# Hybrid delta-net and window-attention block on one Trainium2 core: x's loads behind the branches, decays moved, last norm in two passes, and two projections that pass once over their weights

## The chip, the cores and the metric

The kernel runs on 1 core of one Trainium2 chip. The metric is device time in microseconds (us) of one execution. The profiled execution is one run of the program with the hardware profiler; its rows give, for each instruction, the engine, the start and the duration. Engines: PE is TensorE (matmuls; PEld is its weight load), DVE is VectorE, ACT is ScalarE, POOL is GpSimd, SP is SyncE, whose queue issues nearly all transfers.

## The reference

One layer over 2048 tokens of width 1024, in float32, with two causal mixers side by side:

```
h = x @ w_in                                   # q, k, v, z, beta, decay | q, k, v, z | 2 gates
a: q,k,v = silu(short_conv(h)); gated delta rule in chunks (4 heads of 128)
   u, w come from the inverse of a unit lower triangular matrix per chunk
   o_a = rmsnorm(o_a) * silu(z)
b: 8 query heads of 64, 2 key heads, rope on a quarter, window of 128, a sink per head
   o_b = softmax(band) @ v * silu(z)
merged = sigmoid(gate_a) * (o_a @ w_branch[0]) + sigmoid(gate_b) * (o_b @ w_branch[1])
y = layernorm(alpha * x + merged @ w_out) * ln_g + ln_b
```

## The kernel before

The sequence goes in four chunks of 512 tokens. In the code `T` is 512 and `NB` is 4, the blocks of 128 tokens in a chunk; `KT` is 8, the blocks of 128 along the width. Every large product is made of three fp32r matmuls (L179, L180, L181 in `prods`): each operand is split into a high part and a low part, and high by high, high by low and low by high are summed in PSUM. I call such a group of three a triple.

**Weights and x.** In chunk 0 a weight quarter comes raw from HBM (L159), ACT rounds it to its high part (L160), DVE subtracts (L161), and the split form is stored to a scratch tensor `kw_...` (L145); the later chunks load that form (L156). There are three raw buffers (`W_RAW`) and four split buffers `wb` (`W_SPLIT`). x of the next chunk takes the same raw buffers (`load_x`, L217 to L219).

**Order.** PE's order is written by hand. The strings `ORDER_FIRST` and `ORDER` list the dense pieces of a chunk (`kv`, `w0`, `w1` the query projections, `g` gates, `p` the output projection of the chunk before, and so on). Between them stand background tasks, spawned with a latency (`LAT_...`) on a model clock: `front`, `levels`, `back` of a delta-rule head, `attend` of the window attention, `decays`. The class `Order` puts a step of such a task into PE's stream when the model clock has passed its due time. `st.finish(name)` moves the model clock on until the named task is done, so that its steps then stand back to back. The other engines' orders are made by a list scheduler.

**What the change touches.**
- `decays` makes the decay tables from `ba`: cumulative sums with two matmuls (L293, L294), four small transposes (L308) and a row form `GT` of 8 rows. `front` spreads a row of `GT` over 128 partitions with one matmul (L382) whose stationary operand is `sel`.
- `back` is a serial chain over the four blocks of a head: L504, DVE L506, L509, DVE L511, L512 and L515, DVE L516, L517, and the next block's L504 needs the state that L516 wrote. Dense triples between them cover the trips to DVE.
- `attend` makes for each block the scores (L598, L599), a softmax on DVE and ACT (L606 to L618), transposes of it (L625) and the product with v (L633).
- `window_q` projects queries, block pair by block pair: the four weight quarters are kept in `wb` for the second pair. Rope (L889 on ACT, L893 to L895 on DVE) follows, then `query_rows` transposes (L572). `project` does the same for the output projection with weights `kw_o`.
- `inverse` is a chain on DVE (L943, L944) between transfers: L404 to L406 out and in, L432 to `scrp`, L445 back as `p_` for L457.
- `last_project` ends the program with the last chunk's output projection and its norm: L757, statistics, POOL's power (L878), L764 on DVE beside L762 on ACT, L765, and L766 on POOL for one half and DVE for the other.
- `start` splits the first x and the first three weights as they arrive.

Of the kernel before, what the change touches and what calls it, by code (L numbers as in the profile page):

```python
# [39 lines left out]
LAT_INV, LAT_B, LAT_S, LAT_N, LAT_SM, LAT_D, LAT_M, LAT_K, LAT_Q, LAT_Y, LAT_F, LAT_W = 29600, 2700, 2300, 7700, 9200, 11000, 9000, 1400, 7900, 8300, 4100, 2300  # L40
# [23 lines left out]
def build(tc, xt, xn, wk, wg, par, lnp, cst, out, seq=2048):  # L64
    nc = tc.nc
    NCH = seq // T
    with ExitStack() as ctx:
# [67 lines left out]
        sel = const.tile([8, NH], F32R, name="sel")  # L135
        nc.vector.tensor_copy(sel, selt)
# [37 lines left out]
        def prods(ps, terms, first=True, last=True):  # L174

            n = len(terms) - 1
            cost = PE_R * ps.free_size() / 512
            for i, (sh, sl, mh, ml) in enumerate(terms):
                nc.tensor.matmul(ps, sh, mh, start=(first and i == 0), stop=False)  # L179
                nc.tensor.matmul(ps, sh, ml, start=False, stop=False)  # L180
                nc.tensor.matmul(ps, sl, mh, start=False, stop=(last and i == n))  # L181
                if cost * 3 * (i % 2 + 1) > 1000 or i == n:
                    yield cost * 3 * (i % 2 + 1)
# [12 lines left out]
        def prod_tc(pss, blocks, ah, al, ww, load=None):  # L196

            for g, (wh, wl) in enumerate(ww):
                if load:
                    load(2 * g + 1)  # L200
                for ps, b in zip(pss, blocks):
                    yield from prods(ps, [(tok(ah[2 * g + k], b), tok(al[2 * g + k], b), wh[:, k], wl[:, k])
                                          for k in range(2)], g == 0, g == 3)

        def kept(ww, into):
            for w in ww:
                into.append(w)
                yield w
# [14 lines left out]
        def start(c):  # L223
# [6 lines left out]
            for k in range(KT):  # L230
# [6 lines left out]
                if not k % 4:  # L237
                    wb = [pw.tile([P, 2, 528], F32R, name="wb", bufs=W_SPLIT)[:, :, :512] for _ in FIRST]
                    wh, wl = ([b[:, n] for b in wb] for n in range(2))
                    for i in range(3):  # L240
                        nc.vector.tensor_copy(wh[i], first[i + 3 * (k // 4)])
                        nc.vector.tensor_tensor(wl[i], first[i + 3 * (k // 4)], wh[i].bitcast(F32), ALU.subtract)
                        keep((FIRST[i], k // 4), wb[i])
# [41 lines left out]
        def decays(c, ba):  # L285
# [23 lines left out]
            c.GT = sm.tile([8, T], F32R, name="GT", bufs=1)  # L309
            nc.scalar.activation(c.GT, psr[:8], AF.Copy)  # L310
# [45 lines left out]
        def front(c, h):  # L356
# [25 lines left out]
            nc.tensor.matmul(psR, sel[:, h:h + 1].to_broadcast([8, P]), c.GT, start=True, stop=True)  # L382
# [165 lines left out]
        def window_q(c, gp):  # L548
# [4 lines left out]
            ww, more = [], quarters([f"q{gp}{i}" for i in range(2)])  # L553
            for b0 in (0, 2):
                pss = [mm.tile([P, T], F32, name="mm")[:, :256] for _ in range(2)]
                yield from prod_tc(pss, (b0, b0 + 1), c.xh, c.xl, ww if b0 else kept(more, ww), lambda k: load_x(c, k))
                if b0:
                    st.finish("qT0")
                qr = [pa.tile([P, 256], F32, name="kr") for _ in range(2)]
                for b, ps in enumerate(pss):  # L560
                    rope(nc, sm, qr[b], ps, 4, cos[:, c.i * NB + b0 + b], sin[:, c.i * NB + b0 + b])
                st.spawn(f"qT{b0}", query_rows(c, b0, qr), LAT_Q)
# [114 lines left out]
        def project(c, eg):  # L677
# [3 lines left out]
            ww, more = [], quarters([f"o{eg}{i}" for i in range(2)])  # L681
# [6 lines left out]
            for b2 in range(2):  # L688
                yield from prod_tc([ps[:, b2] for ps in pss], (b2, 2 + b2), c.mh, c.ml, ww if b2 else kept(more, ww))
# [3 lines left out]
        def norm_factors(c, bst, bufs=None):  # L693
# [6 lines left out]
            if bufs:  # L700
                return rs, mv[:, 0:1]
            nm = sm.tile([P, 1], F32, name="lnm")
            nc.vector.scalar_tensor_tensor(nm, mv[:, 0:1], -1.0, rs, ALU.mult, ALU.mult)
            return rs, nm

        def layer_norm(c):
            fs = []
            for b in range(NB):
# [4 lines left out]
                rs, mu = norm_factors(c, bst, NB)  # L713
# [20 lines left out]
        def last_project(c):  # L734
# [9 lines left out]
            for b in range(NB):  # L744
# [51 lines left out]
        for i in range(NCH):  # L796
# [223 lines left out]
```

## Time and profile before

| what | us |
|---|---|
| median of 3 runs | 1695.29 (1693.77 to 1695.6) |
| profiled execution, its own time | 1688.99 |
| its span in the profile | 1687.2 |
| PE busy | 1619.6 (96% of the span) |
| DVE busy | 976.0 (58%) |
| ACT busy | 600.8 (36%) |
| POOL busy | 88.9 (5%) |

The profile page counts an engine as busy while one of its instructions runs. PE's matmuls are pipelined and their ends are modelled, so the distance from one start to the next tells more than a duration. The column PEclk is the share of TensorE's full clock that was granted; 0.5 is the lower of its two levels.

### The profile page before, as it was taken

What the parts mean: (1) busy time and instruction counts of PE and PEld (TensorE: products, weight loads), DVE (VectorE), ACT (ScalarE), POOL (GpSimd) and SP (SyncE); (2) the same over time, 40 slices, a digit from 0 to 9 for tenths busy, and PEclk for the clock granted to TensorE, in tenths of its full rate; (3) what the DMA queues carried; (4) which work ended last, traced back from release to release, by engine and by line L of the source; (5) the groups of instructions that cost most, each with busy time, mean ns of one, the idle gap of its engine ahead of it and who ended that gap; (6) DMA issues with size and microseconds to landing.
All of it is one profiled execution on the core that took longest, in us unless ns stands there. A gap on an engine that the chain in (4) does not pass through costs nothing.

```text
span 1687.2 us, 26971 instructions
## 1 busy us (share of the span) xinstructions
PE 1619.6 (96%) x9846; PEld 1366.6 (81%) x9846; DVE 976.0 (58%) x3015; ACT 600.8 (36%) x1692; POOL 88.9 (5%) x138
## 2 busy tenths in 40 slices
PE   9999999899899999999999999999999999999997
PEld 6878877787788778788888778878888878888787
DVE  6676686548748665433746774623482867462255
ACT  4464456424313633432311453333230244233110
POOL 0100000000001001000000000000000100000001
PEclk9999999999989999999999999999999999999999
DMA  8866584676857446556655835645656664464862
GB/s 307 265 223 198 180 272 154 207 237 218 280 199 221 133 145 176 157 146 224 197 178 182 245 120 150 178 144 176 207 176 193 221 185 122 149 197 138 285 207 76
DMA packets 189157, 323.37 MB, mean 192 GB/s; under 512 B 31072, under 2 KB 45408, under 8 KB 188896
## 3 DMA queue, kind: packets, MB, share of 16 engines
q1 hardware_dynamic: 185184, 316.40, 59.3%
q0 software_dynamic: 3840, 5.25, 1.5%
q8 instruction: 78, 1.28, 0.3%
q14 instruction: 55, 0.45, 0.1%
HBM read 244.97 MB, written 71.37 MB: 187 GB/s over the span
## 4 chain that ended last, share of the span: by engine, by line
PE 79%; DMA 8%; DVE 8%; ACT 2%; issue 1%; SPq 1%; POOL 0%; DVEq 0%; ACTq 0%
PE mm L179 22%; PE mm L181 21%; PE mm L180 21%; PE pp L633 2%; DMA s<-in_lnp 2%; PE pp L625 1%; DMA wb<-kw_o 1%; DMA w<-in_wg 1%; DMA wb<-kw_zb 1%; PE pp L598 1%; PE pd L509 1%; PE pd L504 1%; PE pd L393 1%; PE pp L599 1%; DMA wb<-kw_b 1%
## 5 line engine op out<-in xcount | busy, mean ns | idle before, releaser
L179 PE MATMUL mm<-xh,wb 128*128 128x512 f32 x1128 | 467.1, 414 | 2.0 <-DMA wb<-kw_zb 1.6
L181 PE MATMUL mm<-xh,wb 128*128 128x512 f32 x1128 | 445.4, 395 | 0.0
L180 PE MATMUL mm<-xl,wb 128*128 128x512 f32 x1128 | 444.2, 394 | 0.0
L179 PEld LDWEIGHTS mm<-xh,wb 128*128 128x128 f32 x1128 | 213.1, 189 | 50.3 <-issue 8.9
L181 PEld LDWEIGHTS mm<-xh,wb 128*128 128x128 f32 x1128 | 212.3, 188 | 49.9
L180 PEld LDWEIGHTS mm<-xl,wb 128*128 128x128 f32 x1128 | 213.8, 190 | 38.0
L179 PE MATMUL mm<-wb,xh 128*128 128x256 f32 (+1 forms) x384 | 115.1, 300 | 3.2 <-DVE rope L893 2.9
L179 PE MATMUL mm<-wb,s 128*128 128x256 f32 x384 | 112.1, 292 | 5.5 <-DMA wb<-kw_o 5.3
L180 PE MATMUL mm<-wb,xh 128*128 128x256 f32 (+1 forms) x384 | 109.1, 284 | 0.0
L181 PE MATMUL mm<-wb,s 128*128 128x256 f32 x384 | 109.0, 284 | 0.0
L180 PE MATMUL mm<-wb,s 128*128 128x256 f32 x384 | 108.9, 284 | 0.0
L181 PE MATMUL mm<-wb,xl 128*128 128x256 f32 (+1 forms) x384 | 108.6, 283 | 0.0
L161 DVE TENSOR_TENSOR wb<-w,wb 128x512 fp32r<-128x512 f32 (+1 forms) x110 | 75.7, 690 | 56.2 <-ACT wb L160 53.9
L160 ACT ACTIVATE wb<-w 128x512 fp32r<-128x512 f32 (+1 forms) x110 | 68.9, 628 | 84.8 <-PE mm L181 47.2
L179 PEld LDWEIGHTS mm<-wb,s 128*128 128x128 f32 x384 | 73.6, 192 | 8.3 <-DMA wb<-kw_o 5.2
L943 DVE TENSOR_TENSOR xt<-su,xi 128x16 f32<-128x16 f32 (+15 forms) x256 | 76.4, 298 | 5.4
L179 PEld LDWEIGHTS mm<-wb,xh 128*128 128x128 f32 x384 | 73.2, 191 | 5.8 <-issue 5.4
L944 DVE TENSOR_REDUCE xi<-xt 128x8 f32<-128x16 f32 (+15 forms) x256 | 74.8, 292 | 5.1
L611 ACT ACTIVATE s<-s,nm 128x256 f32<-128x256 f32 (+1 forms) x128 | 62.6, 491 | 39.8 <-DVE nm L608 39.8
L180 PEld LDWEIGHTS mm<-wb,s 128*128 128x128 f32 x384 | 73.6, 192 | 0.1
L181 PEld LDWEIGHTS mm<-wb,s 128*128 128x128 f32 x384 | 73.5, 192 | 0.0
L317 ACT ACTIVATE xs<-mm 128x512 f32<-128x512 f32 x45 | 26.8, 596 | 131.0 <-PE mm L181 129.7
(665 smaller groups left out, 3045.6 us busy)
## 6 DMA issues: line engine op xcount, KB each, us to landing
wb<-kw_h SPq DMA_DIRECT2D x96, 512.0 KB, 4.1
wb<-kw_g SPq DMA_DIRECT2D x96, 512.0 KB, 3.9
w<-in_wg SPq DMA_DIRECT2D x106, 256.0 KB, 4.1
wb<-kw_b SPq DMA_DIRECT2D x48, 512.0 KB, 4.1
wb<-kw_o SPq DMA_DIRECT2D x36, 512.0 KB, 4.5
kw_h<-wb SPq DMA_DIRECT2D x32, 512.0 KB, 3.9
kw_g<-wb SPq DMA_DIRECT2D x32, 512.0 KB, 3.4
wb<-kw_q SPq DMA_DIRECT2D x24, 512.0 KB, 3.9
```

The lines of the kernel that those rows point to most:

```text
L160: nc.scalar.activation(hi, raw, AF.Copy)
L161: nc.vector.tensor_tensor(lo, raw, hi.bitcast(F32), ALU.subtract)
L179: nc.tensor.matmul(ps, sh, mh, start=(first and i == 0), stop=False)
L180: nc.tensor.matmul(ps, sh, ml, start=False, stop=False)
L181: nc.tensor.matmul(ps, sl, mh, start=False, stop=(last and i == n))
L317: nc.scalar.activation(xs[:, 3:], ps, AF.Copy)
L393: nc.tensor.matmul(psKK[:, b], k4[:, b], k4[:, b], start=True, stop=True)
L504: nc.tensor.matmul(ps, k4[:, b], S[:, h], start=True, stop=True)
L611: nc.scalar.activation(ss[v][:, g, k0:], ss[v][:, g, k0:], AF.Exp, bias=nm[:, v, g:g + 1], scale=0.125, accum_out=su[:, v, g:g + 1])
L633: nc.tensor.matmul(psY[64 * v:64 * v + 64], c.vs[b + kb][:, 64 * v:64 * v + 64], pTs[v][:, kb], start=(kb == kbs[0]), stop=(kb == 1))
L943: nc.vector.tensor_tensor(tx[:, :, :, :n], u, x, ALU.mult)
L944: nc.vector.tensor_reduce(xi[:, :, i:i + 2], tx[:, :, :, :n], AX.X, ALU.add)
```

## The change

Five things change. The query projection `window_q` and the output projection `project` go once over their four weight quarters (`prod_all`): each quarter is multiplied with all four token blocks, two blocks to a PSUM bank, with all four sums open. The next chunk's x is loaded one piece behind each `branch_b` product, and no longer all in front of them. `decays` becomes due later (`LAT_Y` 11500 for 8300), and `sel` and `GT` have 128 rows, of which 120 are zero. The last norm takes two fused DVE passes per half, without ACT and POOL. In `start` POOL makes the low parts of the first weights in place of DVE.

```
-LAT_INV, LAT_B, LAT_S, LAT_N, LAT_SM, LAT_D, LAT_M, LAT_K, LAT_Q, LAT_Y, LAT_F, LAT_W = 29600, 2700, 2300, 7700, 9200, 11000, 9000, 1400, 7900, 8300, 4100, 2300
+LAT_INV, LAT_B, LAT_S, LAT_N, LAT_SM, LAT_D, LAT_M, LAT_K, LAT_Q, LAT_Y, LAT_F, LAT_W = 29600, 2700, 2300, 7700, 9200, 11000, 9000, 1400, 7900, 11500, 4100, 2300
...
-        sel = const.tile([8, NH], F32R, name="sel")
-        nc.vector.tensor_copy(sel, selt)
+        sel = const.tile([P, NH], F32R, name="sel")
+        GT = const.tile([P, T], F32R, name="GT")
+        for t in (sel, GT):
+            nc.gpsimd.memset(t.bitcast(F32), 0.0)
+        nc.vector.tensor_copy(sel[:8], selt)
...
+        def prod_all(pss, ah, al, ww, load=None):
+            for g, (wh, wl) in enumerate(ww):
+                if load:
+                    load(2 * g + 1)
+                for b in (0, 2, 1, 3):
+                    yield from prods(pss[b // 2][:, b % 2], [(tok(ah[2 * g + k], b), tok(al[2 * g + k], b), wh[:, k], wl[:, k])
+                                                             for k in range(2)], g == 0 and not b % 2, g == 3, True)
...
-                        nc.vector.tensor_tensor(wl[i], first[i + 3 * (k // 4)], wh[i].bitcast(F32), ALU.subtract)
+                        nc.gpsimd.tensor_tensor(wl[i], first[i + 3 * (k // 4)], wh[i].bitcast(F32), ALU.subtract)
...
-            c.GT = sm.tile([8, T], F32R, name="GT", bufs=1)
-            nc.scalar.activation(c.GT, psr[:8], AF.Copy)
+            nc.scalar.activation(GT[:8], psr[:8], AF.Copy)
...
-            nc.tensor.matmul(psR, sel[:, h:h + 1].to_broadcast([8, P]), c.GT, start=True, stop=True)
+            nc.tensor.matmul(psR, sel[:, h:h + 1].to_broadcast([P, P]), GT, start=True, stop=True)
...
-            ww, more = [], quarters([f"q{gp}{i}" for i in range(2)])
+            pss = [mm.tile([P, 2, 256], F32, name="mm") for _ in range(2)]
+            yield from prod_all(pss, c.xh, c.xl, quarters([f"q{gp}{i}" for i in range(2)]), lambda k: load_x(c, k))
             for b0 in (0, 2):
-                pss = [mm.tile([P, T], F32, name="mm")[:, :256] for _ in range(2)]
-                yield from prod_tc(pss, (b0, b0 + 1), c.xh, c.xl, ww if b0 else kept(more, ww), lambda k: load_x(c, k))
                 if b0:
                     st.finish("qT0")
...
-            for b2 in range(2):
-                yield from prod_tc([ps[:, b2] for ps in pss], (b2, 2 + b2), c.mh, c.ml, ww if b2 else kept(more, ww))
+            yield from prod_all(pss, c.mh, c.ml, quarters([f"o{eg}{i}" for i in range(2)]))
...
-                rs, nm = norm_factors(c, bst)
-                for hs in (slice(0, 512), slice(512, D)):
-                    if hs.start:
-                        nc.scalar.activation(r[:, hs], r[:, hs], AF.Identity, scale=rs, bias=nm)
-                    else:
-                        nc.vector.tensor_scalar(r[:, hs], r[:, hs], rs, nm, ALU.mult, ALU.add)
-                    nc.vector.tensor_tensor(r[:, hs], r[:, hs], lg[:, 0, hs], ALU.mult)
-                    (nc.vector if hs.start else nc.gpsimd).tensor_tensor(r[:, hs], r[:, hs], lg[:, 1, hs], ALU.add)
+                rs, mu = norm_factors(c, bst)
+                halves = slice(0, 512), slice(512, D)
+                for hs in halves:
+                    nc.vector.scalar_tensor_tensor(r[:, hs], r[:, hs], mu, lg[:, 0, hs], ALU.subtract, ALU.mult)
+                for hs in halves:
+                    nc.vector.scalar_tensor_tensor(r[:, hs], r[:, hs], rs, lg[:, 1, hs], ALU.mult, ALU.add)
                     nc.sync.dma_start(out=out[t0:t0 + P, hs], in_=r[:, hs])
...
-            if i < NCH - 1:
-                load_x(nxt, KT - 1)
             for d in range(KT):
                 st.dense([branch_b(c, d)])
+                if i < NCH - 1:
+                    load_x(nxt, d)
```

In the changed kernel the line numbers are higher by 5 to 13: the triple is L184 to L186, the chain of `back` is L517, L522, L525, L528, L530, the scores are L610 and L611, the softmax's transposes L637, the query transposes L584.

SP's queue at the branches of chunk 0 stands so before (in_xt is x, in_wg a raw weight, kw_b the store of a split one):

```order
L145 DMA kw_g14_1_3674<-wb_3669 256x1x512
L217 DMA w_3752<-in_xt 128x512
L145 DMA kw_g15_0_3696<-wb_3691 256x1x512
L217 DMA w_3756<-in_xt 128x512
L145 DMA kw_g15_1_3729<-wb_3724 256x1x512
L217 DMA w_3762<-in_xt 128x512
L217 DMA w_3766<-in_xt 128x512
L217 DMA w_3772<-in_xt 128x512
L217 DMA w_3776<-in_xt 128x512
L217 DMA w_3782<-in_xt 128x512
L217 DMA w_3786<-in_xt 128x512
L159 DMA w_3791<-in_wg 128x512
```

With the change the same place reads:

```order
L163 DMA w_3730<-in_wg 128x512
L149 DMA kw_g15_0_3682<-wb_3677 256x1x512
L231 DMA w_3752<-in_xt 128x512
L149 DMA kw_g15_1_3707<-wb_3702 256x1x512
L163 DMA w_3757<-in_wg 128x512
L149 DMA kw_b0_1_3734<-wb_3729 256x1x512
L231 DMA w_3791<-in_xt 128x512
L149 DMA kw_b1_1_3761<-wb_3756 256x1x512
L163 DMA w_3796<-in_wg 128x512
L231 DMA w_3823<-in_xt 128x512
L163 DMA w_3828<-in_wg 128x512
```

The first weight of the branches stood behind eight loads of x; now it stands ahead of them, and x and weights take turns.

PE at the second query projection of chunk 1 stands so before, at the end of the projection (128x256 triples) and the start of the next product (128x512):

```order
L504 MATMUL pd<-S,k 128x128
...
L181 MATMUL mm<-wb,xl 128x256
L572 MATMUL pp<-ct,kr 128x128 x4
L509 MATMUL pd<-bt,q__6404 128x128
L512 MATMUL pd<-S,qd 128x128
L179 MATMUL mm<-xh,wb 128x512
...
L181 MATMUL mm<-xh,wb 128x512
L515 MATMUL pd<-wc,ktl 128x128
```

With the change it reads:

```order
L186 MATMUL mm<-wb,xl 128x256
L522 MATMUL pd<-bt,q__6439 128x128
L525 MATMUL pd<-S,qd 128x128
L528 MATMUL pd<-wc,ktl 128x128
L530 MATMUL pd<-wc,dt 128x128
L517 MATMUL pd<-S,k 128x128
L584 MATMUL pp<-ct,kr 128x128 x4
L522 MATMUL pd<-bt,q__6439 128x128
L525 MATMUL pd<-S,qd 128x128
L184 MATMUL mm<-xh,wb 128x512
```

Four triples stood between L504 and L509 and four more between L512 and L515; now five steps of the chain follow one another with only the transposes L584 between.

PE in chunk 1 ahead of `k3`, where the head's chain is finished, stands so before, from the last product ahead of the softmax's transposes (between the scores and this piece stand ten triples and two links of the chain):

```order
L181 MATMUL mm<-xh,wb 128x512
L504 MATMUL pd<-S,k 128x128
L625 MATMUL pp<-ct,s 128x128 x8
L509 MATMUL pd<-bt,q__5700 128x128
L512 MATMUL pd<-S,qd 128x128
L633 MATMUL pp<-pT,vb 64x256 x4
L515 MATMUL pd<-wc,ktl 128x128
L517 MATMUL pd<-wc,dt 128x128
```

With the change, from the last score on:

```order
L611 MATMUL pp<-kTl_145,qT_5520 128x256
L184 MATMUL mm<-xh,wb 128x512
...
L186 MATMUL mm<-xh,wb 128x512
L517 MATMUL pd<-S,k 128x128
L522 MATMUL pd<-bt,q__5694 128x128
L525 MATMUL pd<-S,qd 128x128
L528 MATMUL pd<-wc,ktl 128x128
L530 MATMUL pd<-wc,dt 128x128
L637 MATMUL pp<-ct,s 128x128 x4
```

Two triples are now between the last score and the head's last block, and that block's chain and the first transposes follow without a dense product between. Chunks 2 and 3 have the same piece.

## Rows read from the trace of the kernel before

**Rows 1.** The page, part 1: busy us (share of span) xinstructions.

```profile
PE 1619.6 (96%) x9846; PEld 1366.6 (81%) x9846; DVE 976.0 (58%) x3015; ACT 600.8 (36%) x1692; POOL 88.9 (5%) x138
```

**Rows 2.** PE's waits: us in total, times, longest us.

```profile
PE pd L457 <- DMA p__4900<-scrp: 8.4, 1, 8.4
PE mm L179 <- ACT wb L160: 7.2, 1, 7.2
PE mm L179 <- DMA wb<-kw_o: 5.3, 7, 1.9
PE pd L509 <- DVE bt L506: 5.3, 6, 1.5
PE pd L464 <- DVE q__968 L450: 3.6, 1, 3.6
PE mm L179 <- DVE rope L893: 2.9, 1, 2.9
PE pd L382 <- DVE ktl L372: 2.6, 4, 1.1
PE pd L293 <- DVE gg L922: 2.6, 1, 2.6
PE pd L457 <- DMA p__2747<-scrp: 2.4, 1, 2.4
...
PE mm L179 <- DMA wb<-kw_zb: 1.6, 2, 0.9
...
PE pp L598 <- DVE x__2861 L459: 1.2, 1, 1.2
...
PE pd L478 <- ACT x__2861 L451: 0.9, 1, 0.9
```

**Rows 3.** Stretches: us, then busy of PE, PEld, DVE, ACT, POOL, PEclk, DMA share.

```profile
44.00:54.00 10.00, 7.10 (x47) 6.93 (x47) 7.45 (x38) 3.58 (x13) 1.54 (x3) 0.83 0.91 314
119.00:132.00 13.00, 9.03 (x66) 7.34 (x65) 6.86 (x30) 7.63 (x25) 1.54 (x2) 0.87 0.29 88
245.00:262.00 17.00, 12.01 (x93) 9.04 (x92) 10.41 (x32) 10.13 (x35) 0.20 (x1) 0.87 0.45 144
332.00:345.00 13.00, 5.85 (x23) 4.64 (x22) 5.71 (x9) 5.30 (x9) 0.00 (x0) 0.74 0.67 215
```

**Rows 4.** SP's timeline at chunk 0's branches: start, us, line, transfer, times.

```profile
323.13 12.63 SPq L217 DMA_DIRECT2D w<-in_xt  x6
336.03 4.46 SPq L159 DMA_DIRECT2D w<-in_wg  x3
```

**Rows 5.** PE's timeline around the first L382: start, us, line, shape.

```profile
64.67 0.39 PE L180 MATMUL mm<-xl,wb 128*128 128x512 f32 x1
64.90 0.39 PE L181 MATMUL mm<-xh,wb 128*128 128x512 f32 x1
65.22 0.49 PE L382 MATMUL pd<-GT,sel 8*128 8x512 f32 x1
65.64 0.50 PE L179 MATMUL mm<-xh,wb 128*128 128x512 f32 x1
```

**Rows 6.** PE and DVE timelines, a link of `back` in chunk 2.

```profile
985.39 0.49 PE L504 MATMUL pd<-S,k 128*128 128x128 f32 x2
986.12 0.34 DVE L506 SCALAR_TENSOR_TENSOR bt<-pd,neG,vt 128x128 f32<-128x128 f32 x1
```

**Rows 7.** The timeline from the last score of a block to its softmax, chunk 1.

```profile
577.39 0.28 PE L599 MATMUL pp<-kTl,qT 128*128 128x256 f32 x1
584.13 1.70 ACT L618 ACTIVATE s<-s,sum 128x256 f32<-128x256 f32 x4
```

**Rows 8.** The chain that ended last, its end: start us, us, what.

```profile
1679.25 0.17 DVE lnm L703
...
1680.03 1.30 DVE yBl L765 x2
1681.33 0.02 issue
1681.35 1.63 DVE yBl L766
```

**Rows 9.** POOL's addition in the last norm: duration ns min/median/max, first and last start.

```profile
L766 POOL TENSOR_TENSOR yBl<-yBl,yAh x2: 1641/1660/1680, 1670.5 to 1680.8; 128x512 f32<-128x512 f32 x2
```

More of the change, by code (lines that the diff above doesn't have):

```diff
@@ L172, in quarters, with prods @@
                     yield half_w(name, i, 2)
-        def prods(ps, terms, first=True, last=True):
+        def prods(ps, terms, first=True, last=True, shared=False):
             n = len(terms) - 1
@@ L178, in prods @@
             for i, (sh, sl, mh, ml) in enumerate(terms):
-                nc.tensor.matmul(ps, sh, mh, start=(first and i == 0), stop=False)
-                nc.tensor.matmul(ps, sh, ml, start=False, stop=False)
-                nc.tensor.matmul(ps, sl, mh, start=False, stop=(last and i == n))
+                nc.tensor.matmul(ps, sh, mh, start=(first and i == 0), stop=False, skip_group_check=shared)
+                nc.tensor.matmul(ps, sh, ml, start=False, stop=False, skip_group_check=shared)
+                nc.tensor.matmul(ps, sl, mh, start=False, stop=(last and i == n), skip_group_check=shared)
                 if cost * 3 * (i % 2 + 1) > 1000 or i == n:
@@ L559, in window_q @@
                 qr = [pa.tile([P, 256], F32, name="kr") for _ in range(2)]
-                for b, ps in enumerate(pss):
-                    rope(nc, sm, qr[b], ps, 4, cos[:, c.i * NB + b0 + b], sin[:, c.i * NB + b0 + b])
+                for b in range(2):
+                    rope(nc, sm, qr[b], pss[b0 // 2][:, b], 4, cos[:, c.i * NB + b0 + b], sin[:, c.i * NB + b0 + b])
                 st.spawn(f"qT{b0}", query_rows(c, b0, qr), LAT_Q)
@@ L680, in project @@
                 c.ra = [py.tile([P, 2, D], F32, name=n) for n in ("yBh", "yBl")]
-            ww, more = [], quarters([f"o{eg}{i}" for i in range(2)])
             es = slice(256 * eg, 256 * eg + 256)
@@ L687, in project, with norm_factors @@
                 nc.sync.dma_start(out=xr[bp], in_=xn[t0:t0 + 256, es].rearrange("(b p) e -> p b e", p=P))
-            for b2 in range(2):
-                yield from prod_tc([ps[:, b2] for ps in pss], (b2, 2 + b2), c.mh, c.ml, ww if b2 else kept(more, ww))
+            yield from prod_all(pss, c.mh, c.ml, quarters([f"o{eg}{i}" for i in range(2)]))
             for bp in range(2):
                 nc.vector.scalar_tensor_tensor(c.ra[bp][:, :, es], xr[bp], 2.0 * ALPHA, pss[bp], ALU.mult, ALU.add)
-        def norm_factors(c, bst, bufs=None):
+        def norm_factors(c, bst):
             mv = sm.tile([P, 2], F32, name="mv", bufs=NB)
@@ L699, in norm_factors @@
             rsqrt(nc, sm, rs, va, mhalf)
[L700 to L704, printed above, removed]
+            return rs, mv[:, 0:1]
         def layer_norm(c):
@@ L712, in layer_norm @@
                     nc.vector.bn_stats(bst[:, i], r[:, 512 * i:512 * i + 512])
-                rs, mu = norm_factors(c, bst, NB)
+                rs, mu = norm_factors(c, bst)
                 fs.append((r, rs, mu))
@@ L758, in last_project @@
                         nc.vector.bn_stats(bst[:, e0 + e], r[:, es])
-                rs, nm = norm_factors(c, bst)
-                for hs in (slice(0, 512), slice(512, D)):
-                    if hs.start:
-                        nc.scalar.activation(r[:, hs], r[:, hs], AF.Identity, scale=rs, bias=nm)
-                    else:
-                        nc.vector.tensor_scalar(r[:, hs], r[:, hs], rs, nm, ALU.mult, ALU.add)
-                    nc.vector.tensor_tensor(r[:, hs], r[:, hs], lg[:, 0, hs], ALU.mult)
-                    (nc.vector if hs.start else nc.gpsimd).tensor_tensor(r[:, hs], r[:, hs], lg[:, 1, hs], ALU.add)
+                rs, mu = norm_factors(c, bst)
+                halves = slice(0, 512), slice(512, D)
[3 more added lines that the diff above has]
+                    nc.vector.scalar_tensor_tensor(r[:, hs], r[:, hs], rs, lg[:, 1, hs], ALU.mult, ALU.add)
                     nc.sync.dma_start(out=out[t0:t0 + P, hs], in_=r[:, hs])
```

## Prediction

> **What bounds the kernel now.** I read the page first: PE is busy 96% of the span, 1619.6 us of 1687.2 [rows 1], and no other engine comes near. So a change gains only where it closes a gap of PE's or makes its products shorter, and it loses where it opens one. The change takes no dense product away: each weight quarter still meets each of the four token blocks. So I went to PE's waits next [rows 2], to see which gaps there are and what ends them, then to the windows around the largest ones for the clock that was granted there [rows 3], and last to single places of the timeline, for the lengths of the trips that the new order leaves bare. The reader is to see in rows 2 that the gaps are few and named: 8.4 us for an inverse that came back late, 7.2 for a raw weight, 5.3 and 1.6 for kept weights, 3.6 for DVE's transposes, 2.9 for a rope, 2.6 for the decays. In rows 3 a gap costs more than itself: PEclk over the 13 us around the 7.2 us gap is 0.74, so 0.26 x 13 = 3.4 us of full-speed work were lost beside it; around the 3.6 us gap it is 0.87 over 13 us, 1.7 us; around the rope 0.83 over 10 us, 1.7 us.
>
> **What goes.**
> (a) *x's loads.* At the branches of chunk 0, six loads of x take SP's queue from 323.13 for 12.63 us, and the first branch weight is issued only at 336.03 [rows 4]; PE waits 7.2 us for its split (L160). In the new order that weight stands ahead of the loads. I count the wait and its clock, 7.2 + 3.4 = 10.6. A branch product takes 12 x 0.23 = 2.8 us and now needs two raw tiles of three, one of a weight and one of x; if that falls short, up to 2 us of it come back.
> (b) *Kept weights.* Before, a projection's first pair of blocks used up a quarter in four triples of 256 columns (half of 0.23 each product [rows 5], so 1.4 us) and held all four split buffers until its second pair was through, so the weights behind it came late: L179 waits 5.3 us in seven places for `kw_o` and 1.6 in two for `kw_zb` [rows 2]. With one pass a quarter serves eight triples, 2.8 us, before the next is wanted, and its buffer is free at once. Both go: 6.9.
> (c) *First inverse of chunk 0.* L464 waits 3.6 us for DVE's transposes L450, which stood behind splits, scores and `front`'s work on DVE; in the new order DVE does them ahead of that work. With the clock 3.6 + 1.7 = 5.3.
> (d) *Rope behind kv in chunk 0.* The wait of 2.9 stood behind a split that itself waited for a weight; in the new order DVE's copies out of PSUM come ahead of it. With the clock 2.9 + 1.7 = 4.6.
> (e) *Decays.* L293's wait for `gg`, 2.6, since L293 comes six triples later.
> (f) *Small links* that get dense products between: in chunk 0 those of the third inverse, 1.2 and 0.9, with half of the clock lost there (0.13 x 17 = 2.2, half 1.1), together 3.2; and L382 behind L372, 2.6 in four places, which now has the softmax's work and four triples between. Sum 5.8.
> (g) *128 rows for L382.* From L382's start to the next start are 0.42 us, between two 128-row products of the same width 0.23 [rows 5]; there are 16 of them, 16 x 0.19 = 3.0. The Trainium skill speaks against this: on the page "TensorE: Matmul & The Clock Gate", section "Step-by-step: what each phase is for", throughput is put at N cycles, one column in each, whatever the rows. By it the padding would bring nothing, and the sum would be 3.0 worse. The row decides for me, since the two products differ in nothing else that streams; nothing and 3.0 are the bounds.
> (h) *Tail.* From 1679.25 the last norm takes 3.73 us on DVE, with POOL beside it [rows 8]: L765 two times takes 1.30, but L766 1.63 alone while POOL adds the other half. Four fused passes at 0.65 take 2.6, and the last output leaves 1.1 earlier.
> Sum of what goes: 10.6 + 6.9 + 5.3 + 4.6 + 2.6 + 5.8 + 3.0 + 1.1 = 39.9.
> The largest wait stays: L457 for `p__4900`, 8.4 us. Its inverse is late through DVE and SP in chunk 0, and nothing there is made shorter. It can move by 5 us in either direction, with the splits around it.
>
> **What comes.** The new places come from PE's written order. `st.finish("qT0")` and `st.finish("back1")` move the model clock on over fewer dense products, and steps that had triples between stand back to back.
> (i) *The chain behind the query projections.* A link of `back` runs from L504's start at 985.39 to DVE's end at 986.12 + 0.34 and back to PE, about 1.1 us [rows 6]; already before, such a link was bare six times, 5.3 us in all [rows 2]. In the second query projection of chunks 1 to 3 now three links are bare, with one or two small products between, 0.9 + 0.9 + 0.5 = 2.3, three times 6.9. Chunk 0's second projection has three as well, 2.3. In the four first projections one stands bare or the first L572 waits for the rope, about 1 us each. Sum 13.2; if DVE is busy with a longer instruction at the link, 0.3 more each, and if it is early for lack of other work, 0.2 less: 10 to 18.
> (j) *The softmax ahead of `k3`, chunks 1 to 3.* Before, from the last score at 577.39 to the end of the last L618 (584.13 + 1.70) were 8.4 us [rows 7]; the first L625 needs only the first two of the four L618, some 0.9 less, 7.5. The order before had ten triples and three links there and covered it. Now there are two triples, 6 x 0.23 = 1.4, and two bare links. These links are lost, 2 x 0.95 = 1.9; together with the triples and the chain's last products they cover 3.9, so that up to 3.6 more is bare. In a stalled stretch ACT gets fewer other instructions between the steps of the softmax (in rows 7 it was held up by a new product's copies), and the wait may be 1.2 only; I take 2.4. With the links 4.3, in three chunks 12.9. The stretches of rows 3 lost clock behind waits of 3 us; here the wait is cut into pieces, so half of 1.7 in each chunk, 2.6. Sum 15.5, bounds 9 and 22.
> (k) *Decays moved.* In chunks 0 and 1 the four transposes L308 now directly follow L293 and L294 and wait for DVE's L298: one link of 1.1 each, 2.0.
> (l) *Start.* POOL makes low parts of 128x512; its addition of two such tiles takes 1.66 [rows 9], DVE's 0.65 [rows 8]. The first and the second matmul with a low part come 1.0 later, some of it in what PE waited for anyway: 1.4, bounds 0.5 and 3.
> (m) *Inverses.* In four of the sixteen heads PE now has some 5 us less to do between the inverse's start and L457; the heads before had little to spare, as the waits for `p__4900` and `p__2747` show [rows 2]. I take 2.5, bounds 0 and 12: nothing where DVE's chain is also earlier, 3 to 4 in each of the three later heads where it isn't.
> Two memsets of POOL, five more transfers on SP and the later stores are beside PE's work in chunk 0, where PE has its first dense products; without that cover they would cost under 1 us each.
> Sum of what comes: 13.2 + 15.5 + 2.0 + 1.4 + 2.5 = 34.6.
>
> **The sum.** 34.6 - 39.9 = -5.3. The profiled execution took 1688.99, 1.8 beyond its span, so 1683.7 for one like it. It was 6.3 under the median of 1695.29; from the median the sum gives 1690.0. Both sides of the sum are seven times as large as the result, and that sets the range.
>
> **Rivals.**
> *Faster, 1675.* The links and the softmax are covered after all, since the engines that are asked have less queued in front of them: (i) and (j) cost their lower halves, 9 in place of 28.7, and (m) nothing. Then -39.9 + 9 + 2.0 + 1.4 = -27, cut by the 2 of (a) and 5 of things not foreseen: 1675. For it: DVE has 42% idle time and ACT 64% [rows 1], and the gaps in (a) to (d) are measured while the new ones are built from an order. Against it: a chain of back-to-back steps doesn't get shorter than its links.
> *Slower, 1704.* The softmax is the place: if ACT and DVE do the next head's work ahead of it, as in rows 7, each of the three waits is 3.6 with its links and a full clock loss, 1.9 + 3.6 + 1.7 = 7.2, 21.6 in all, and if the second projections then drop the clock too, 3 x 1.7 = 5, with the inverses at 6. That is 13.2 + 21.6 + 5 + 2.0 + 1.4 + 6 = 49.2 against 39.9: +9. It decides from 40 us of new waits on.
> *No gain from the 128 rows, 1693.* A product streams its columns in a time that doesn't depend on its rows, and the 0.42 of rows 5 is a cost of something else around L382, such as its weight load. Then (g) falls out and the sum is -2.3. It is the rule of the Trainium skill's page named at (g); the trace of before doesn't agree with it, at 0.42 against 0.23.
>
> **How the numbers follow.** A measurement of this kernel can tell about 0.2%, 3.4 us. The forecast (-5.3, own range 1684 to 1696) has 0.42: 0.27 faster, 0.13 same, 0.02 slower. The faster rival has 0.26. The slower one has 0.22. The one without (g) has 0.10: 0.02 faster, 0.07 same, 0.01 slower. That makes 0.55 faster, 0.20 same and 0.25 slower. The range reaches to both rivals, 1674 to 1704, which leaves out about 2 in 10.
>
> **What would show it.** In the profile after: no wait of L184 for L160 at 330 to 340 us, and PEclk 1.0 there (a); no rows for `kw_o` among PE's waits (b); L463 no longer waited for by L477 at 120 us (c); L395's starts 0.23 apart from the next (g). Against these stand new rows for L522, L528 and L517 behind DVE, some 1 us each, in twenty-odd places (i), and L637 behind L630 three times (j). The forecast is wrong if waits for L637 are over 4 us or none, if an inverse's `p_` is waited for in more than two heads, or if x's loads come late enough to be waited for by the next chunk's first product.

## The result and the profile after

The changed kernel takes 1671.78 us (median of 4 runs, 1668.77 to 1673.48) against 1695.44 for the kernel before (4 runs, 1693.77 to 1700.42): a ratio of 0.9855, 95% interval 0.9832 to 0.9879, so some 24 us faster. The prediction was 1690.0 with a range from 1674 to 1704; the direction was right, the size was not, and the time lies 2 us under the range. Of the rivals the faster one, 1675, came nearest.

The profiled executions differ by less: a span of 1670.4 us against 1687.2, 16.8. The profile of before that I predicted from was one of the shortest executions of that kernel (more at the run before_again).

The page's first part and the waits of PE, of the kernel after (us in total, times, longest us); they answer to [rows 1] and [rows 2]:

```profile
PE 1618.9 (97%) x9846; PEld 1368.2 (82%) x9846; DVE 969.3 (58%) x3005; ACT 596.2 (36%) x1688; POOL 92.9 (6%) x142
```

```profile
PE pp L637 <- ACT s L630: 6.4, 3, 2.1
PE pd L522 <- DVE bt L519: 5.9, 9, 2.2
PE pd L517 <- DVE S L529: 5.0, 4, 2.5
PE pp L584 <- DVE rsq L884: 3.4, 1, 3.4
...
PE pd L395 <- DVE ktl L385: 2.4, 3, 1.2
PE pd L528 <- DVE wc L524: 2.2, 8, 0.6
PE pd L322 <- DVE ghl L312: 2.0, 2, 1.6
PE pd L470 <- DMA p__4808<-scrp: 1.9, 1, 1.9
PE pd L470 <- DMA p__1886<-scrp: 1.6, 1, 1.6
```

The list counts a wait from the modelled end of the product before it. Of the waits in [rows 2], those for the branch weight, for `kw_o`, for the transposes of the first inverse and for `kw_zb` are gone, and the wait for the inverse in chunk 1, `p__4900` before and `p__4808` now, is 1.9 in place of 8.4. What leads the list now are links that the new order leaves bare: the softmax (L637), the delta chain (L522, L517, L528) and the query transposes (L584).

Stretches of the kernel after (us, busy of PE, PEld, DVE, ACT, POOL, PEclk, DMA share, GB/s); the first, second and fourth answer to [rows 3]:

```profile
44.00:54.00 10.00, 9.25 (x79) 9.08 (x78) 8.84 (x41) 6.03 (x19) 2.06 (x4) 1.00 0.97 329
119.00:132.00 13.00, 13.00 (x83) 10.70 (x82) 7.51 (x27) 9.49 (x29) 0.19 (x1) 1.00 0.56 161
160.00:180.00 20.00, 17.71 (x111) 13.57 (x110) 8.70 (x27) 5.05 (x17) 1.73 (x3) 0.83 0.47 144
245.00:262.00 17.00, 17.00 (x105) 13.80 (x104) 12.35 (x38) 11.77 (x36) 1.22 (x2) 1.00 0.53 172
330.00:345.00 15.00, 12.77 (x54) 10.22 (x53) 7.86 (x15) 5.05 (x8) 0.00 (x0) 0.89 0.72 238
436.00:456.00 20.00, 17.97 (x170) 17.01 (x170) 7.25 (x15) 4.34 (x9) 0.19 (x1) 0.91 0.83 265
500.00:520.00 20.00, 15.65 (x77) 13.19 (x78) 14.48 (x64) 5.43 (x19) 2.10 (x3) 0.83 0.74 232
585.00:600.00 15.00, 12.13 (x58) 9.80 (x57) 11.91 (x52) 7.10 (x25) 1.54 (x2) 0.89 0.22 70
```

The three places around 50, 125 and 250 us are closed and run at full clock: at 245 to 262 PE was busy 12.01 of 17 us, now 17.00. The new low places are 160 to 180 (an inverse, `p__1886`), 500 to 520 (chunk 1's first query projection) and 585 to 600 (the softmax ahead of `k3`). Each has its own loss of clock, as a stall had before: 0.17 x 20 = 3.4 us at 160 to 180 and at 500 to 520, 0.11 x 15 = 1.7 at 585 to 600.

The tail, in the chain that ended last (start us, us, what), answers to [rows 8]:

```profile
1663.94 0.15 DVE va L707
1664.09 1.32 DVE yBl L768 x2
...
1665.90 0.75 DVE yBl L770
1666.65 0.66 DVEq L1020
```

The first of the two fused passes, L768, needs only the mean, so DVE runs it while POOL makes the power; only the second pass waits for the scale. From the last product to the end were 10.6 us, now 7.7.

### The profile page after: what moved, and what is told of

Read it like the earlier page. It is cut to its first block, busy times and chain, and to the rows that moved or that the text cites. A ratio compares the mean times of both kernels' runs of the same rounds, so it can differ in the third digit from the quotient of the medians.

```text
span 1670.4 us, 26939 instructions
## 1 busy us (share of the span) xinstructions
PE 1618.9 (97%) x9846; PEld 1368.2 (82%) x9846; DVE 969.3 (58%) x3005; ACT 596.2 (36%) x1688; POOL 92.9 (6%) x142
## 3 DMA queue, kind: packets, MB, share of 16 engines
q8 instruction: 78, 1.28, 0.3%
## 4 chain that ended last, share of the span: by engine, by line
PE 82%; DVE 7%; DMA 7%; ACT 2%; issue 1%; SPq 1%; POOL 0%; DVEq 0%; ACTq 0%; POOLq 0%
PE mm L184 22%; PE mm L186 22%; PE mm L185 22%; PE pp L645 2%; PE pp L637 2%; DMA s<-in_lnp 2%; DMA w<-in_xt 1%; PE pp L610 1%; PE pp L611 1%; PE pd L432 1%; DVE wb L165 1%; PE pd L517 1%; PE pd L528 1%; DMA xl<-kw_o 1%; PE pd L406 1%
## 5 line engine op out<-in xcount | busy, mean ns | idle before, releaser
L184 PE MATMUL mm<-xh,wb 128*128 128x512 f32 x1128 | 468.6, 415 | 0.0
L186 PE MATMUL mm<-xh,wb 128*128 128x512 f32 x1128 | 448.0, 397 | 0.0
L186 PEld LDWEIGHTS mm<-xh,wb 128*128 128x128 f32 x1128 | 213.7, 189 | 50.3
L184 PEld LDWEIGHTS mm<-xh,wb 128*128 128x128 f32 x1128 | 214.5, 190 | 45.6 <-issue 6.5
L184 PE MATMUL mm<-wb,xh 128*128 128x256 f32 (+1 forms) x384 | 113.5, 296 | 1.8 <-DVE kr L899 0.9
L184 PE MATMUL mm<-wb,s 128*128 128x256 f32 x384 | 110.4, 287 | 0.0
L186 PE MATMUL mm<-wb,xl 128*128 128x256 f32 (+1 forms) x384 | 108.7, 283 | 0.0
L186 PE MATMUL mm<-wb,s 128*128 128x256 f32 x384 | 108.4, 282 | 0.0
L184 PEld LDWEIGHTS mm<-wb,xh 128*128 128x128 f32 x384 | 72.9, 190 | 2.7 <-issue 2.5
L184 PEld LDWEIGHTS mm<-wb,s 128*128 128x128 f32 x384 | 73.1, 190 | 0.8
L185 PEld LDWEIGHTS mm<-wb,xh 128*128 128x128 f32 x384 | 72.9, 190 | 0.5
L186 PEld LDWEIGHTS mm<-wb,s 128*128 128x128 f32 x384 | 73.0, 190 | 0.0
```

The costliest lines, as they stand in the source:

```text
L185: nc.tensor.matmul(ps, sh, ml, start=False, stop=False, skip_group_check=shared)
```

## The experiments

Each time stands beside runs of the kernel before on the same chip; ratios are to that kernel, with 95% intervals. The changed kernel's is 0.9855.

**before_again: the kernel before, unchanged.**

> The kernel before, once more, for its profile on another occasion. Its profiled execution took 1689.0 us, its other runs 1693.8 to 1700.4. If the difference lies in the waits for transfers, this profile shows the waits for p__4900, for the raw branch weight and for kw_o longer by some 6 us together than 8.4, 7.2 and 5.3. If it is a matter of the clock alone, the waits are the same within 1 us and the mean granted clock is lower by 0.004.

It took 1696.92 us, with a span of 1695.2 and the mean clock at 0.986 for 0.989. The three named waits did not grow (8.3, 7.2 and 4.3 for `kw_o`). Others did: 1.6 at L598 for `yb`, 1.8 in the last projection for `kw_o`, the second with lower clock behind it, and some tenths at `kw_b`:

```profile
PE mm L179 <- DMA wb<-kw_b: 2.4, 3, 1.7
...
PE pp L180 <- DMA yAl<-kw_o: 1.8, 1, 1.8
PE pp L598 <- DVE yb L638: 1.6, 1, 1.6
```

So the execution that I read had a few stalls less than this one. My guess had the wrong waits. Of the 8.0 us between the two spans PE stands still for 4.9 and is busy 3.1 longer (1622.7 us for 1619.6), so stalls and clock both have a part. That most executions are like this one, and that this is why the medians differ by more than the profiles, fits but is not shown by one profile.

The clock differs by itself too. Here are the first two stretches of [rows 3] in this execution:

```profile
44.00:54.00 10.00, 7.14 (x61) 6.97 (x60) 7.81 (x45) 3.81 (x14) 1.19 (x3) 1.00 0.84 294
119.00:132.00 13.00, 9.07 (x61) 7.59 (x62) 6.50 (x28) 7.33 (x24) 1.54 (x2) 0.74 0.22 64
```

PE stands still as long as before in both, but the clock is 1.00 for 0.83 in the first and 0.74 for 0.87 in the second. So the same wait cost 1.7 us of clock in one execution and nothing in the other, and the second 1.7 and 3.4.

**x_ahead and b_x_behind: the place of x's loads, in the changed kernel and alone in the one before.**

```
x_ahead:     + load_x(nxt, KT - 1)      ahead of the loop over the branches
             - load_x(nxt, d)           in it
b_x_behind:  the reverse, in the kernel before
```

> The changed kernel with x's eight loads again ahead of the branches. The wait for the first branch weight comes back, 7.3 and 3.4 of clock, while the link waits of 2.4 and 1.0 and their clock 1.7, which stand there now, go under it: net 5 to 7, 1677 to 1679. If the moved loads are also what shortened the wait for p__4900 (theory B), 8 to 10 more: 1686 to 1689.

> The kernel before with x's loads behind the branches alone. The wait of 7.2 for the first branch weight and its clock 3.4 go; as in the changed kernel up to 5 come back as links of the delta chain, which stood under that wait: 5 to 10 under the kernel before, 0.994 to 0.997. If the loads now collide with the splits of the branches: no gain.

x_ahead: 1676.02 us, 0.9881 (0.9864 to 0.9898). The wait for the branch weight is back with 6.1 us, and the inverse's wait stays small (1.5): the first theory of that text, by 0.0026 of the ratio, about 4 us for the 5 to 7 expected; the intervals of the two kernels overlap. b_x_behind: 1686.02 us, 0.9936 (0.9906 to 0.9967), 11 us, somewhat more than expected. Its profile shows why: the wait for the inverse fell too, from 8.4 to 2.6.

```profile
PE pd L457 <- DMA p__4900<-scrp: 2.6, 1, 2.6
```

**p_twice and b_p_once: the output projection's passes.**

```
p_twice:   - yield from prod_all(pss, c.mh, c.ml, quarters(...))
           ...
           + for b2 in range(2): yield from prod_tc([ps[:, b2] for ps in pss], (b2, 2 + b2), ..., ww if b2 else kept(more, ww))
b_p_once:  the reverse, in the kernel before
```

> The changed kernel with its output projection again in two passes over kept weights. Theory A: the 8.4 us wait for p__4900 of the kernel before came from the raw weights of this projection, which SP, ACT and DVE had to handle at twice the pace just then; it comes back with its clock, 8 to 11 us, and the waits for kw_o with 6: 1686 to 1690. Theory B: that wait went because x's loads were moved away; then only kw_o comes back: 1677 to 1679.

> The kernel before with the output projection alone once over its weights. Theory A: the waits for kw_o go, 6, and the wait for p__4900 falls from 8.4 to 3 to 5 with some of its clock, 5 to 7: 11 to 13 under the kernel before, a ratio of 0.9925 to 0.9935. Theory B (p__4900 needs another part of the change): 6 under it, 0.9965.

p_twice: 1686.02 us, 0.9933 (0.9909 to 0.9958), 13 us lost against the changed kernel: L184 waits 8.8 us for `kw_o` in twelve places, and the inverse's wait is 4.3. b_p_once: 1686.35, 0.9935 (0.9916 to 0.9955), 11 us won: no wait for `kw_o` is left, and 5.2 for `p__4900`. Theory A in both, with a part of the inverse's wait only. How the projection makes the inverse late is to be read on SP's timeline (start us, us, line, transfer), first of the kernel before:

```profile
454.77 0.58 SPq L432 DMA_DIRECT2D scrp<-xi  x1
455.40 0.97 SPq L159 DMA_DIRECT2D w<-in_wg  x1
456.47 0.83 SPq L687 DMA_DIRECT2D s<-in_xn  x1
457.42 0.52 SPq L145 DMA_DIRECT2D kw_o<-wb  x1
458.04 0.55 SPq L687 DMA_DIRECT2D s<-in_xn  x1
458.94 0.87 SPq L159 DMA_DIRECT2D w<-in_wg  x1
460.14 0.52 SPq L145 DMA_DIRECT2D kw_o<-wb  x1
460.77 2.75 SPq L445 DMA_DIRECT2D p__4900<-scrp  x4
```

and of the kernel after:

```profile
431.31 0.78 SPq L445 DMA_DIRECT2D scrp<-xi  x1
432.14 1.04 SPq L698 DMA_DIRECT2D s<-in_xn  x2
433.27 0.52 SPq L149 DMA_DIRECT2D kw_o<-wb  x1
433.84 0.60 SPq L163 DMA_DIRECT2D w<-in_wg  x1
435.87 1.84 SPq L458 DMA_DIRECT2D p__4808<-scrp  x4
```

Between the inverse's way out and its way back stood two raw weights and two stores of split ones, now one of each. The store at 460.14 waits for DVE's split of a weight that was asked for 7 us earlier, and the return stands behind it. That costs little by itself, since the way out landed only 5.3 us after its issue, at 460.07 (now 4.5); the four transfers back take 2.75 us on the queue, now 1.84, and from the last of them to PE's first product pass 2.4 us, now 2.0. So the way back is 2.7 us shorter in all, and the wait fell by 6.5; where the rest comes from stands under the step that failed, below.

**q_twice: the query projection in two passes, in the changed kernel.**

```
-            yield from prod_all(pss, c.xh, c.xl, quarters(...), lambda k: load_x(c, k))
...
             for b0 in (0, 2):
...
+                yield from prod_tc(pss, (b0, b0 + 1), c.xh, c.xl, ww if b0 else kept(more, ww), ...)
```

> The changed kernel with its query projection again in two passes, everything else as changed. Theory A: the new waits of the changed kernel (softmax ahead of k3 3 x 5.3 with the clock, links of the delta chain and of the query transposes some 12 to 15) come from the shorter order around the query projection alone. Then they go, about 2 us of waits for kw_zb come back, and the time is 1645 to 1655 us. Theory B: they come from the later decays (LAT_Y), which shift the whole delta chain of a chunk; then they stay, and the time is 1672 to 1676.

1664.38 us, 0.9811 (0.9791 to 0.9831), faster than the changed kernel by 0.0044, some 7 us, between the times of the two theories. No wait for L637 is left, so theory A has the cause of those waits: the one pass made them, not the later decays, which this run keeps. But it lost elsewhere: in chunk 0 inverses are waited for with 4.9 and 3.4 us, and matched product by product its profile is 15 us behind the changed kernel's at the end of chunk 0's branches and 5 ahead at the end. So the one pass is worth 15 in chunk 0 and costs 20 behind it.

**q_mixed: one pass in chunk 0, two passes in chunks 1 to 3.**

```
+            if not c.i:
                 (one pass)
+            else:
                 (two passes)
```

> The changed kernel with its query projections once over the weights in chunk 0 and in two passes in chunks 1 to 3. From the records of the run with two passes everywhere: up to the branches of chunk 0 that run was 15 us behind the changed kernel, and behind them it won 20. Theory A (the two effects are separate, each of its own chunks' order): 1649 to 1655 us, no waits for L637, no inverse waited for 4 us in chunk 0. Rival (the loss in chunk 0 and the gain later are one thing, heads shifted against each other): 1662 to 1668, as with two passes everywhere.

1657.17 us, 0.9765 (0.975 to 0.9779): faster than both kernels, by 15 us against the changed one (0.0090 of 1695), and 2 us above the span that theory A gave. The two effects are separate. Its stretches at the two places, to hold against those of the kernel after (15.65 and 12.13 busy, 0.83 and 0.89):

```profile
585.00:600.00 15.00, 13.89 (x105) 10.39 (x104) 7.43 (x27) 5.78 (x18) 1.54 (x2) 1.00 0.38 113
500.00:520.00 20.00, 19.54 (x109) 16.64 (x109) 17.63 (x69) 5.98 (x15) 3.12 (x5) 1.00 0.99 336
```

**b_q0_once, b_q0_w0, b_q0_w1: in the kernel before, chunk 0's query projections alone in one pass, both, only the first, only the second.**

```
+            if not c.i:             (w0: and not gp, w1: and gp)
                 (one pass)
```

> The kernel before with the query projections of chunk 0 alone once over their weights. If the one pass is what shortened chunk 0's inverses (waits for L464 behind L450, for p__2747 and the group behind it, and part of p__4900): 9 to 14 us under the kernel before, a ratio of 0.992 to 0.995, with the 7.2 wait for the first branch weight still there. If it needs the other parts: no difference, or 3 to 5 slower by the links behind the projections.

> The kernel before with only the first query projection of chunk 0 once over its weights. Local theory: a projection's raw weights, taken at half the pace, give DVE room for the inverse that runs beside that projection. Then the waits that follow this projection change: L464 behind L450 at 119 us (3.8 and its clock 1.7), while the group at 245 to 262 (6 and clock) and p__4900 (8.4) stay: 5 to 7 under the kernel before, 0.996. Shift theory: any one pass moves all later steps on the model clock and changes them all, 0.988 to 0.993.

> The kernel before with only the second query projection of chunk 0 once over its weights. Local theory: the waits of the group at 245 to 262 go (p__2747 2.4, 1.3, 0.4, 1.0 and clock 3.4, together 8 to 10), those at 119 stay; 0.994 to 0.995. DVE then has 7 or 8 splits instead of 11 between the inverse's in-transfer and its out-transfer. Shift theory: 119 as well, and p__4900 falls, 0.988 to 0.991.

Both: 1678.27 us, 0.988 (0.9838 to 0.9922), 20 us by the medians, more than expected; by the spans 12 against the profile of before and 20 against before_again. First only: 1694.92, 1.0001 (0.9983 to 1.0019). Second only: 1689.44, 0.9962 (0.9941 to 0.9982). In the profile of the first only, L464's wait at 119 us is gone, as the local theory has it, but 3.7 for the second head's inverse (`p__1870`) have come in its place, 8.4 us of wait for the chunk 1 inverse stay and a new one of 4.8 stands in the delta chain. In that of the second only, the 119 us wait stays at 3.8, the group at 245 to 262 is gone and the chunk 1 inverse's is 4.0. The waits that go are those of the local theory, but for the chunk 1 inverse's, whose fall the shift theory had; the times are those of neither. Alone they give 0 and 6, together 20. That the shift of the later steps decides what is left of a local gain would fit, but no run separates it.

What happens locally can be read on DVE between an inverse's way in and its way out, chunk 0's third head (line, operation, count, busy us, mean ns, idle before), of the kernel before, 208 to 241 us:

```profile
L161 DVE TENSOR_TENSOR wb<-w,wb 128x512 fp32r<-128x512 f32 x11 | 7.5, 686 | 4.3 <-ACT wb L160 4.3
L943 DVE TENSOR_TENSOR xt<-su,xi 128x16 f32<-128x16 f32 (+15 forms) x16 | 4.8, 298 | 0.2
L944 DVE TENSOR_REDUCE xi<-xt 128x8 f32<-128x16 f32 (+15 forms) x16 | 4.7, 291 | 0.2
```

and with both in one pass, 204.1 to 232.4 us:

```profile
L161 DVE TENSOR_TENSOR wb<-w,wb 128x512 fp32r<-128x512 f32 x7 | 4.8, 690 | 2.0 <-ACT wb L160 2.0
L963 DVE TENSOR_TENSOR xt<-su,xi 128x16 f32<-128x16 f32 (+15 forms) x16 | 4.8, 298 | 0.2
L964 DVE TENSOR_REDUCE xi<-xt 128x8 f32<-128x16 f32 (+15 forms) x16 | 4.7, 292 | 0.2
```

The inverse's own 32 steps take 9.5 us in both. Eleven splits with their waits take 11.8 us of DVE's time before, seven take 6.8; these 5 us are about what the inverse comes earlier, from 32.8 us to 28.3.

**laty8300 and q_mixed_laty: the decays' due time.**

```
- LAT_Y = 11500
+ LAT_Y = 8300      (in the changed kernel, and in q_mixed)
```

> The changed kernel with the decays due as early as before. If the later time is worth something: L307 waits for the decays' last DVE step again, 2.6 us in chunk 1, and its transposes L322 no longer wait (2.0): within 3 us of 1672. If it also set where the head's links fall: more than 5 us away from it.

> The version with one pass in chunk 0 and two passes in chunks 1 to 3, with the decays due as early as before. In the changed kernel the early decays gained 5 by the middle of chunk 1 and lost 8 in chunks 2 and 3 at the one-pass query projections. If that loss belongs to the one pass, this version wins 3 to 5: 1652 to 1654. If the later decays are needed with two passes as well: 1657 to 1662.

In the changed kernel: 1675.72, 0.9875 (0.9859 to 0.989), 3 us slower by the ratio, with intervals that overlap, and between the two cases that were expected. L637 still waits 6.4, which again rules the decays out as its cause; L528 waits 6.3 in place of 2.2, and the inverses of the second head and of chunk 1 are waited for with 3.3 and 3.2. In q_mixed: 1654.18, 0.9757 (0.9719 to 0.9795), against 0.9765 (0.975 to 0.9779): the medians are 3 us apart, the intervals overlap, so this is open. q_mixed and its two variants are the fastest here.

**rows8, old_norm, q_mixed_start: the three small parts undone.**

```
rows8:          - GT = const.tile([P, T], ...)        + GT = const.tile([8, T], ...)    (sel too)
old_norm:       the norm of before in last_project
q_mixed_start:  - nc.gpsimd.tensor_tensor(wl[i], ...)  + nc.vector.tensor_tensor(wl[i], ...)   (in q_mixed)
```

> The changed kernel with sel and GT of 8 rows. If the 8-row product is really slower: its start to the next start is 0.42 us against 0.24, 16 times, and the time 2 to 4 us above the changed kernel's, 1674 to 1676. If something else around it was: 0.24 and no difference.

> The changed kernel with the last norm of before. The changed kernel's profile has its first pass on DVE while POOL works out the power, so its tail is 7.7 us behind the last product, against 10.6: 3 us slower, 1674 to 1676. If the output transfers set the tail: 1 slower.

> The version with one pass in chunk 0 and two passes in chunks 1 to 3, with the first weights' low parts on DVE as before. If POOL's longer subtraction is what PE waits for in the first 20 us (0.6 each in three places and lower clock behind them): 1 to 2.5 under that version, 1655 to 1656. If DVE's queue is then late for the first x: no difference or slower.

rows8: 1681.9, 0.9899 (0.9867 to 0.9932), some 7 us slower by the ratio, with intervals that overlap; its four runs spread from 1673.3 to 1683.4. With 8 rows the next product starts 0.42 later again. With 128 rows it is 0.24 (start us, us):

```profile
63.04 0.39 PE L186 MATMUL mm<-xh,wb 128*128 128x512 f32 x1
63.27 0.40 PE L395 MATMUL pd<-GT,sel 128*128 128x512 f32 x1
63.51 0.39 PE L184 MATMUL mm<-xh,wb 128*128 128x512 f32 x1
```

That holds at ten of the sixteen places; at the other six it is 0.32. The product ahead of it is left sooner as well: 0.23 from L186's start to L395's, where [rows 5] has 0.32 from L181's to L382's. So the 8 rows are what made it slow, and the rule of N cycles whatever the rows (the Trainium skill, "TensorE: Matmul & The Clock Gate", section "Step-by-step: what each phase is for") does not hold for this fp32r product: 0.42 us at 8 rows [rows 5], 0.24 at 128. What rows8 loses beyond that is, among others, a stall of 1.6 us for `yb` at 99 us, which other executions had and the changed kernel's profile had not, and 4.9 us of waits at L528 for 2.2. old_norm: 1672.71, 0.9848 (0.9805 to 0.989), no difference in the time; in its profile the tail is 10.6 us again, so the 2.9 are there, less than these times can tell. q_mixed_start: 1657.9, 0.9758 (0.9711 to 0.9804), no difference.

## Why the prediction was wrong, by its steps

**The step that failed** is the one that closes the first list: "The largest wait stays ... nothing there is made shorter." It fell from 8.4 us to 1.9. The clock behind it was 3.5 before (0.38 x 9.1, the line below) and 1.8 after (0.09 x 20), so some 8 us went at this place. Three parts of the change each shorten the wait when made alone: x behind the branches to 2.6, the output projection's one pass to 5.2, chunk 0's query projections to 2.5.

```profile
465.90:475.00 9.10, 8.98 (x80) 8.61 (x81) 1.79 (x6) 0.80 (x3) 0.00 (x0) 0.62 0.01 3
```

What each part does to this inverse can be read from three starts: its first transfer out of SBUF (L404, now L417), DVE's result on its way out (L432, now L445, both shown at b_p_once) and PE's first product with it (L457, now L470). Of the kernel before and of the kernel after:

```profile
413.53 2.62 SPq L404 DMA_DIRECT2D scrm<-m  x4
465.92 0.31 PE L457 MATMUL pd<-p__4900,m 32*32 32x32 f32 x2 [8.35 <-DMA p__4900<-scrp]
```

```profile
393.82 1.86 SPq L417 DMA_DIRECT2D scrm<-m  x4
439.73 0.24 PE L470 MATMUL pd<-p__4808,m 32*32 32x32 f32 x2 [1.87 <-DMA p__4808<-scrp]
```

The same three starts in the other runs give this table (us):

| | before | after | b_p_once | b_x_behind | b_q0_once | p_twice | x_ahead |
|---|---|---|---|---|---|---|---|
| until DVE's result goes out | 41.2 | 37.5 | 41.9 | 35.2 | 37.1 | 37.4 | 36.9 |
| way back, until PE's first product | 11.2 | 8.4 | 7.5 | 9.4 | 9.2 | 10.8 | 8.7 |
| PE's wait | 8.4 | 1.9 | 5.2 | 2.6 | 2.5 | 4.3 | 1.5 |

The output projection's one pass shortens the way back alone, in the kernel before (11.2 to 7.5) and in the changed one (10.8 to 8.4). x's loads and chunk 0's query projections shorten what lies ahead of it, by 6.0 and 4.1, and the way back by some 2. The gains do not add up: with x's loads in front again the changed kernel's inverse is no later. Why loads that stand some 80 us ahead of it move this inverse is not shown. I had looked at DVE's work for that inverse alone, and neither at when DVE can begin it nor at what SP's queue holds on its way back. Step (b) has a part of the same cause in it, the raw weights at half the pace, and I counted only PE's own waits for kept weights.

**The clock of the long waits.** I took 3.4 for the clock at (a), from the whole stretch; but the lower level began while PE still stood, and what fell on products is 1.5 (0.30 x 4.9), so (a) is 8.7 and not 10.6:

```profile
340.10:345.00 4.90, 4.81 (x17) 3.92 (x18) 2.11 (x4) 1.30 (x3) 0.00 (x0) 0.70 0.81 270
```

**(f) and (m): the inverses of chunk 0.** For the third inverse I took 3.2; the stretch 245 to 262 gives 5.0 of busy time and 2.2 of clock. The 5.0 hold the inverse's own wait of 2.4, which is 0.4 now, at 239 us; so 6.8. The other half of (f) did not come: L395 still waits 2.4 behind L385, where 2.6 was to go. For (m) I took a loss of 2.5, since the heads had less of PE's work over them; but the third inverse itself became faster, 32.8 to 28.3 with chunk 0's one pass alone, since fewer splits stand on DVE beside it, and so did the one of chunk 1. The sign was wrong. A loss of the kind I feared did come in the second head, the 1.6 of `p__1886` with 3.4 of clock. With the 0.4 an inverse's `p_` is now waited for in three heads, one more than the prediction had allowed.

**(h)** The tail gained 2.9 for 1.1: the first pass goes under POOL's power, which I overlooked.

**The base.** I set the sum against the profile and carried it over to the median. The gap between the medians of the two kernels is 7 us larger than between the two profiles; the profile of before was 6.3 under its median, that of the changed kernel 0.5 above.

**Right, and by their own sizes** (waits from here on by starts, 0.2 us more for each than in the list): (j), 12.9 and 2.6 of clock expected, is 3 x (0.6 + 0.4 + 2.3) = 9.9 at L522, L528 and L637 in their three places, and 3 x 1.7 of clock, 15.0. (i), 13.2 expected: by the list the waits of L522, L517, L528 and L584 in the kernel after are 16.5 in all; without the 2.0 of (j) and the 3.1 at the branches 11.4, some 18 with the smaller rows and 5.1 of clock, against 6.3 for L509 and L504 before, so 12. They are unevenly spread: 2.3 for the second projections was too much (0.8 to 1.3 each), 1 for the first ones too little, since in chunk 1 L584 waited 3.4 for the rope behind other work on DVE. (g) is confirmed and somewhat larger, 2.6 to the next start and 1.6 ahead of it in the sixteen places, 4.2 for 3.0. (a) was right in what it removes; the links that stood under that wait then showed, 2.4 and 1.0 with 1.7 of clock, so that its sign, PEclk 1.0, did not come (0.89). (c) is right but for 1.5 that L610 now waits there, (d) fell to two waits of 0.7 and 0.9, (e) was given back by (k), 2.0 with 1.7 of clock. (l) shows no difference in the time, in q_mixed_start.

**What stays open.** Between the two profiles PE stands still 16.1 us less and is busy 0.7 less. By an estimate from the granted clock, less what fell on waits and the tail, the lower level cost products some 12 us before and 20 after; (g) gives back 4. So some 5 us of the gain lie in no wait that the list names, and I can't say where.

**The rivals.** "Faster" had nearly the right time for a wrong reason: the new links and the softmax are not hidden, they cost what I had said. The gains were larger. "No gain from the 128 rows" is out by rows8's profile and the 4.2 of (g).

## What to carry to other kernels

A weight stream that is consumed at half the pace can pay beyond its own waits: a serial chain that shares DVE's and SP's queues with its splits and stores can get shorter. Not every one does: of the first five inverses three became 5 to 7 us shorter, from the first transfer out to the last landing, and two 0.5 and 1.1 us longer. Before a wait is said to stay, read what stands on each queue between its cause and its end, and which of that the change slows down or removes. An edit that helps in the chunk where weights are split can hurt where they are only loaded: here one pass in chunk 0 and two passes elsewhere beat both kernels, 1657 us against 1672 and 1695.

## What the runs showed of the hardware beyond that

A stall cut in pieces can lose clock as one piece does: in the kernel after, waits of 0.6, 0.4 and 2.3 us within 5 us ahead of `k3` were followed each of the three times by 3.4 us at the lower level, 1.7 us lost. It need not: what a wait costs in clock differed between two executions of the same kernel (before_again). POOL's subtraction of 128x512 took 1.28 us in the start (the median of six), less than its addition in the last norm [rows 9].
